# Macro tiles of 1024 x 2048 with 8 KB load rows in a quarter-turn kernel

## The chip, the cores and the metric

The kernel runs on one core of one Trainium2 chip (the other cores are not used by it). The metric is the device time of one execution in microseconds (us). Each kernel was run several times; medians are given with their range. All runs named here were in the fast state. The profile is one traced execution. Ratios are the mean time of one kernel's fast runs over that of the other's fast runs of the same rounds, so they are not quite the ratio of the medians that are quoted.

## The reference

```python
x = np.random.randn(8192, 8192).astype(np.float32);  k = 1
def reference(x, k):
    return np.rot90(x, k)          # out[i, j] = x[j, 8191 - i]
```

That is a transpose with the output rows in reverse order: 268 MB are read and 268 MB are written, and nothing is computed.

## The kernel before

It works in macro tiles, that is, blocks of the matrix that are loaded, transposed and stored together; here they have 1024 rows x 1024 columns. Each is loaded as two tiles of 2 MB, VectorE reverses the columns within each block of 128, TensorE transposes blocks of 128 x 128 into PSUM (the memory that TensorE writes to), ScalarE copies PSUM to an output tile, and ScalarE's queue stores 2 MB at a time. Both directions move rows of 1024 floats, that is, contiguous runs of 4 KB.

```python
QT = 4; PT = 4; S = 512; K = 2
a_pool, r_pool, o_pool: bufs=3 each, tiles of 2 MB;  psum_pool: bufs=2
for RB2 in range(n_rb2):
    for CB2 in range(n_cb2):
        ar_list = []
        for t in range(K):
            a_big = a_pool.tile([P, QT, K * S], dt, tag="a_big")
            src = x[r_base + t*S : r_base + (t+1)*S, c_base : c_base + K*S].rearrange("(q r) c -> r q c", q=QT)
            nc.sync.dma_start(out=a_big[:], in_=src)
            ar_big = r_pool.tile([P, QT, K * S], dt, tag="ar_big")
            nc.vector.tensor_copy(out=ar_big..., in_=a_big...[:, :, ::-1])      # cut
            ar_list.append(ar_big)
        for s in range(K):
            o_big = o_pool.tile([P, PT, K * S], dt, tag="o_big")
            for t in range(K):
                ... 16 transposes into psum_t ...                               # cut
                nc.scalar.copy(o_big[:, :, t*S : (t+1)*S], psum_t[:])
            nc.scalar.dma_start(out=dst, in_=o_big[:])
```

Of the kernel before, what the change touches and what calls it, by code (L numbers as in the profile page):

```python
# [1 line left out]

# [5 lines left out]

P = 128  # L10


@with_exitstack
def kernel(
    ctx: ExitStack,
    tc: tile.TileContext,
    x: bass.AP,
    k: bass.AP,
    out: bass.AP,
):  # L20
    nc = tc.nc
    assert k == 1, f"only k=1 supported, got {k}"

    N, M = x.shape
    dt = x.dtype

    QT = 4
    PT = 4
    S = 512
    K = 2  # L30

    n_rb2 = N // (K * S)
    n_cb2 = M // (K * S)

    consts = ctx.enter_context(tc.tile_pool(name="consts", bufs=1))
    ident = consts.tile([P, P], dt)
    make_identity(nc, ident)

    a_pool = ctx.enter_context(tc.tile_pool(name="a_pool", bufs=3))
    r_pool = ctx.enter_context(tc.tile_pool(name="r_pool", bufs=3))  # L40
    o_pool = ctx.enter_context(tc.tile_pool(name="o_pool", bufs=3))
    psum_pool = ctx.enter_context(tc.tile_pool(name="psum", bufs=2, space=bass.MemoryType.PSUM))

    for RB2 in range(n_rb2):
        for CB2 in range(n_cb2):
            c_base = CB2 * K * S
            r_base = RB2 * K * S

            ar_list = []
            for t in range(K):  # L50
                a_big = a_pool.tile([P, QT, K * S], dt, tag="a_big")
                src = x[
                    r_base + t * S : r_base + (t + 1) * S, c_base : c_base + K * S
                ].rearrange("(q r) c -> r q c", q=QT)
                nc.sync.dma_start(out=a_big[:], in_=src)  # L55

                ar_big = r_pool.tile([P, QT, K * S], dt, tag="ar_big")
                nblk = QT * K * S // P
                rev_src = a_big.rearrange("r q (b m) -> r (q b) m", m=P)[:, :, ::-1]
                nc.vector.tensor_copy(  # L60
                    out=ar_big.rearrange("r q (b m) -> r (q b) m", m=P),
                    in_=rev_src,
                )
                ar_list.append(ar_big)

            for s in range(K):
                cb = K * CB2 + s
                o_big = o_pool.tile([P, PT, K * S], dt, tag="o_big")
                for t in range(K):
                    psum_t = psum_pool.tile([P, PT, QT * P], mybir.dt.float32)  # L70
                    ar_big = ar_list[t]
                    for p in range(PT):
                        w = PT - 1 - p
                        col0 = s * S + p * P
                        for q in range(QT):
                            nc.tensor.transpose(  # L76
                                psum_t[:, w, q * P : (q + 1) * P],
                                ar_big[:, q, col0 : col0 + P],
                                ident,
                            )  # L80
                    nc.scalar.copy(o_big[:, :, t * S : (t + 1) * S], psum_t[:])  # L81

                top = N - S - cb * S
                dst = out[top : top + S, r_base : r_base + K * S].rearrange(
                    "(p m) f -> m p f", p=PT
                )
                nc.scalar.dma_start(out=dst, in_=o_big[:])


# [1 line left out]
_INS = ['x', 'k']  # L91
_OUTS = [((8192, 8192), 'float32')]
#: Inputs that are plain numbers.
_NUMBERS = {'k': 1}


# [26 lines left out]
```

## Time and profile before

| | before |
|---|---|
| time, median of 4 runs | 1285.98 us (1285.63 to 1286.27) |
| DMA rate in mid-kernel | 421 GB/s, engines full in every slice but the last |
| busy: TensorE, ScalarE, VectorE | 56%, 37%, 23% |
| load packets, store packets | 65,536 and 65,536 of 4 KB |

These are lines of the page of the kernel before. DMA is the busy share of the 16 DMA engines in 40 slices, in tenths; GB/s is what they moved; then come packets, queues (q1 is the load queue, q10 the store queue), the chain of waits by line, groups of instructions (busy us, mean ns; idle time before them and what ended it), and the DMA issues (number, size, median us from issue to landing).

```profile
DMA  9999999999999999999999999999999999999998
GB/s 382 422 421 421 421 421 422 421 421 421 421 421 421 421 421 421 421 422 421 420 421 421 421 421 421 421 421 421 422 420 420 421 421 422 421 421 421 421 421 361
DMA packets 135208, 537.48 MB, mean 418 GB/s; under 512 B 4096, under 2 KB 4096, under 8 KB 135168
...
q1 hardware_dynamic: 67584, 268.44, 50.9%
q10 hardware_dynamic: 67584, 268.44, 50.9%
...
DMA a_big<-in_x_dram 88%; DVE ar_big L60 8%; PE psum_t L76 2%; ACT o_big L81 1%; DVEq L60 0%; SPq L55 0%
...
L81 ACT COPY o_big<-psum_t 128x2048 f32<-128x2048 f32 x256 | 469.9, 1868 | 801.5 <-DMA out_dram<-o_big 771.6
L60 DVE COPY ar_big<-a_big 128x4096 f32<-128x4096 f32 x128 | 293.6, 2294 | 970.6 <-DMA a_big<-in_x_dram 816.4
...
a_big<-in_x_dram SPq DMA_DIRECT2D x128, 2048.0 KB, 27.4
out_dram<-o_big ACTq DMA_DIRECT2D x128, 2048.0 KB, 26.1
```

The reader should see that no slice of the DMA line is below 9 until the last, that the engines which compute wait for transfers for most of the time, and that both queues carry the same number of packets. The DMA engines bound the kernel.

The end of the kernel before, as stretches of 4 us (columns: busy us and number of instructions of PE, PEld, DVE, ACT and POOL, then granted TensorE clock, DMA share, GB/s):

```profile
1262.00:1266.00 4.00, 1.66 (x11) 1.69 (x12) 2.19 (x1) 1.87 (x1) 0.00 (x0) 0.88 1.02 421
1266.00:1270.00 4.00, 4.00 (x28) 4.00 (x27) 0.00 (x0) 2.13 (x2) 0.00 (x0) 0.69 0.72 297
1270.00:1274.00 4.00, 1.44 (x14) 1.21 (x12) 0.00 (x0) 3.37 (x2) 0.00 (x0) 1.00 1.00 407
```

There is a hole at 1266 to 1270 us: the last loads have landed, and the blocks that they brought are still being transposed (PE busy all 4.00 us), so there is too little to store.

### The profile page before, as it was taken

What the parts mean: (1) busy time and instruction counts of PE and PEld (TensorE: products, weight loads), DVE (VectorE), ACT (ScalarE), POOL (GpSimd) and SP (SyncE); (2) the same over time, 40 slices, a digit from 0 to 9 for tenths busy, and PEclk for the clock granted to TensorE, in tenths of its full rate; (3) what the DMA queues carried; (4) which work ended last, traced back from release to release, by engine and by line L of the source; (5) the groups of instructions that cost most, each with busy time, mean ns of one, the idle gap of its engine ahead of it and who ended that gap; (6) DMA issues with size and microseconds to landing.
All of it is one profiled execution on the core that took longest, in us unless ns stands there. A gap on an engine that the chain in (4) does not pass through costs nothing.

```text
span 1284.6 us, 9394 instructions
## 1 busy us (share of the span) xinstructions
PE 718.8 (56%) x4096; PEld 662.7 (52%) x4096; DVE 293.6 (23%) x128; ACT 471.1 (37%) x257; POOL 0.7 (0%) x6
## 2 busy tenths in 40 slices
PE   5465564556555565456554565555646556465553
PEld 5455464555544555456454464555645456455553
DVE  2222222222222222222222222222222222222221
ACT  3334433343333433343333433334333343334433
POOL 0000000000000000000000000000000000000000
PEclk9666766776767767776777767767677766776776
DMA  9999999999999999999999999999999999999998
GB/s 382 422 421 421 421 421 422 421 421 421 421 421 421 421 421 421 421 422 421 420 421 421 421 421 421 421 421 421 422 420 420 421 421 422 421 421 421 421 421 361
DMA packets 135208, 537.48 MB, mean 418 GB/s; under 512 B 4096, under 2 KB 4096, under 8 KB 135168
## 3 DMA queue, kind: packets, MB, share of 16 engines
q1 hardware_dynamic: 67584, 268.44, 50.9%
q10 hardware_dynamic: 67584, 268.44, 50.9%
q8 instruction: 32, 0.52, 0.1%
q14 instruction: 8, 0.07, 0.0%
HBM read 268.44 MB, written 268.44 MB: 418 GB/s over the span
## 4 chain that ended last, share of the span: by engine, by line
DMA 88%; DVE 8%; PE 2%; ACT 1%; issue 0%; DVEq 0%; SPq 0%
DMA a_big<-in_x_dram 88%; DVE ar_big L60 8%; PE psum_t L76 2%; ACT o_big L81 1%; DVEq L60 0%; SPq L55 0%
## 5 line engine op out<-in xcount | busy, mean ns | idle before, releaser
L76 PE MATMUL psum_t<-ident,ar_big 128*128 128x128 f32 x4096 | 718.8, 354 | 552.7 <-ACT o_big L81 354.4
L76 PEld LDWEIGHTS psum_t<-ident,ar_big 128*128 128x128 f32 x4096 | 662.7, 188 | 608.5 <-ACT o_big L81 389.5
L81 ACT COPY o_big<-psum_t 128x2048 f32<-128x2048 f32 x256 | 469.9, 1868 | 801.5 <-DMA out_dram<-o_big 771.6
L60 DVE COPY ar_big<-a_big 128x4096 f32<-128x4096 f32 x128 | 293.6, 2294 | 970.6 <-DMA a_big<-in_x_dram 816.4
L81 ACT ACT_TABLE_LOAD x1 | 1.3, 1283 | 0.7 <-PEq L104 0.7
masks.py:199 POOL TENSOR_SCALAR_AFFINE_SELECT ident<-ident 128x128 f32<-128x128 f32 x1 | 0.3, 292 | 0.1
masks.py:197 POOL MEMSET ident<- 128x128 f32 x1 | 0.2, 204 | 0.3 <-POOLq L104 0.3
L104 POOL MEMSET const-bfloat16-1.0<- 128x1 bf16 x1 | 0.1, 102 | 0.0
L104 POOL MEMSET const-uint8-127<- 128x1 uint8 x1 | 0.1, 102 | 0.0
L104 POOL MEMSET const-float32-0.0<- 128x1 f32 x1 | 0.1, 98 | 0.2 <-issue 0.2
L104 POOL MEMSET const-float32-1.0<- 128x1 f32 x1 | 0.1, 98 | 0.0
## 6 DMA issues: line engine op xcount, KB each, us to landing
a_big<-in_x_dram SPq DMA_DIRECT2D x128, 2048.0 KB, 27.4
out_dram<-o_big ACTq DMA_DIRECT2D x128, 2048.0 KB, 26.1
```

What stands on the lines that cost most here:

```text
L60: nc.vector.tensor_copy(out=ar_big.rearrange("r q (b m) -> r (q b) m", m=P), in_=rev_src,)
L76: nc.tensor.transpose(psum_t[:, w, q * P : (q + 1) * P], ar_big[:, q, col0 : col0 + P], ident,)
L81: nc.scalar.copy(o_big[:, :, t * S : (t + 1) * S], psum_t[:])
L104: nc = _bacc.Bacc("TRN2", target_bir_lowering=False, num_devices=1)
```

## The change

The intent: load rows of 8 KB (2048 floats) in place of 4 KB, in 1 MB transfers through a short staging ring of three tiles; keep 16 reversed row tiles (two macro tiles); store 2 MB as before, in rows of 4 KB. The diff, cut to its core:

```diff
+R = 1024
+C = 2048
+RT = R // P        # 8 row tiles of 1 MB
+G = 4096 // R
+PW = 2048 // R
-    r_pool = ctx.enter_context(tc.tile_pool(name="r_pool", bufs=3))
+    r_pool = ctx.enter_context(tc.tile_pool(name="r_pool", bufs=2 * RT))
...
-            for t in range(K):
-                a_big = a_pool.tile([P, QT, K * S], dt, tag="a_big")
-                src = x[...].rearrange("(q r) c -> r q c", q=QT)
-                nc.sync.dma_start(out=a_big[:], in_=src)
+            for t in range(RT):
+                a = a_pool.tile([P, C], dt, tag="a")               # bufs=3
+                nc.sync.dma_start(out=a[:], in_=x[r0 + t * P : r0 + (t + 1) * P, c0 : c0 + C])
+                ar = r_pool.tile([P, C], dt, tag="ar")
+                nc.vector.tensor_copy(out=ar..., in_=a...[:, :, ::-1])
+                rows.append(ar)
...
+            for g0 in range(0, CG, G):
+                o = o_pool.tile([P, G, R], dt, tag="o")            # bufs=3
+                for h in range(0, G, PW):
+                    ... 16 transposes into ps ...
+                    nc.scalar.copy(o[:, G - PW - h : G - h, :], ps[:])
+                nc.scalar.dma_start(out=dst, in_=o[:])
```

More of the change, by code (lines that the diff above doesn't have):

```diff
@@ L10 @@
 P = 128
+R = 1024
+C = 2048
+RT = R // P
+CG = C // P
+G = 4096 // R
+PW = 2048 // R
 @with_exitstack
@@ L25 @@
     dt = x.dtype
-    QT = 4
-    PT = 4
-    S = 512
-    K = 2
-    n_rb2 = N // (K * S)
-    n_cb2 = M // (K * S)
     consts = ctx.enter_context(tc.tile_pool(name="consts", bufs=1))
@@ L39 @@
     a_pool = ctx.enter_context(tc.tile_pool(name="a_pool", bufs=3))
-    r_pool = ctx.enter_context(tc.tile_pool(name="r_pool", bufs=3))
+    r_pool = ctx.enter_context(tc.tile_pool(name="r_pool", bufs=2 * RT))
     o_pool = ctx.enter_context(tc.tile_pool(name="o_pool", bufs=3))
-    psum_pool = ctx.enter_context(tc.tile_pool(name="psum", bufs=2, space=bass.MemoryType.PSUM))
-    for RB2 in range(n_rb2):
-        for CB2 in range(n_cb2):
-            c_base = CB2 * K * S
-            r_base = RB2 * K * S
-            ar_list = []
-            for t in range(K):
-                a_big = a_pool.tile([P, QT, K * S], dt, tag="a_big")
-                src = x[
-                    r_base + t * S : r_base + (t + 1) * S, c_base : c_base + K * S
-                ].rearrange("(q r) c -> r q c", q=QT)
-                nc.sync.dma_start(out=a_big[:], in_=src)
-                ar_big = r_pool.tile([P, QT, K * S], dt, tag="ar_big")
-                nblk = QT * K * S // P
-                rev_src = a_big.rearrange("r q (b m) -> r (q b) m", m=P)[:, :, ::-1]
+    psum_pool = ctx.enter_context(
+        tc.tile_pool(name="psum", bufs=2, space=bass.MemoryType.PSUM)
+    )
@@ L60 @@
+    for r0 in range(0, N, R):
+        for c0 in range(0, M, C):
+            rows = []
+            for t in range(RT):
+                a = a_pool.tile([P, C], dt, tag="a")
+                nc.sync.dma_start(
+                    out=a[:], in_=x[r0 + t * P : r0 + (t + 1) * P, c0 : c0 + C]
+                )
+                ar = r_pool.tile([P, C], dt, tag="ar")
                 nc.vector.tensor_copy(
-                    out=ar_big.rearrange("r q (b m) -> r (q b) m", m=P),
-                    in_=rev_src,
-                )
@@ L64 @@
-                ar_list.append(ar_big)
-            for s in range(K):
-                cb = K * CB2 + s
-                o_big = o_pool.tile([P, PT, K * S], dt, tag="o_big")
-                for t in range(K):
-                    psum_t = psum_pool.tile([P, PT, QT * P], mybir.dt.float32)
-                    ar_big = ar_list[t]
-                    for p in range(PT):
-                        w = PT - 1 - p
-                        col0 = s * S + p * P
-                        for q in range(QT):
+                    out=ar.rearrange("r (b m) -> r b m", m=P),
@@ L76 @@
+                    in_=a.rearrange("r (b m) -> r b m", m=P)[:, :, ::-1],
+                )
+                rows.append(ar)
+            for g0 in range(0, CG, G):
+                o = o_pool.tile([P, G, R], dt, tag="o")
+                for h in range(0, G, PW):
+                    ps = psum_pool.tile([P, PW, R], mybir.dt.float32)
+                    for w in range(PW):
+                        col = (g0 + h + w) * P
+                        for t in range(RT):
                             nc.tensor.transpose(
-                                psum_t[:, w, q * P : (q + 1) * P],
@@ L78 @@
-                                ar_big[:, q, col0 : col0 + P],
+                                ps[:, PW - 1 - w, t * P : (t + 1) * P],
+                                rows[t][:, col : col + P],
                                 ident,
                             )
-                    nc.scalar.copy(o_big[:, :, t * S : (t + 1) * S], psum_t[:])
-                top = N - S - cb * S
-                dst = out[top : top + S, r_base : r_base + K * S].rearrange(
-                    "(p m) f -> m p f", p=PT
+                    nc.scalar.copy(o[:, G - PW - h : G - h, :], ps[:])
@@ L86 @@
+                top = M - c0 - (g0 + G) * P
+                dst = out[top : top + G * P, r0 : r0 + R].rearrange(
+                    "(g m) f -> m g f", g=G
                 )
-                nc.scalar.dma_start(out=dst, in_=o_big[:])
+                nc.scalar.dma_start(out=dst, in_=o[:])
 _INS = ['x', 'k']
```

## The prediction

> **What bounds it now.** The DMA engines. The page's slices show them at 9 in every slice, 421 GB/s nearly throughout; TensorE is busy 56%, ScalarE 37%, VectorE 23%. The chain of waits is 88% loads, and the longest waits of the compute engines name transfers (VectorE 816 us for loads, ScalarE 772 us for stores). So 536.9 MB / 421 GB/s = 1275 us, plus some 9 us of start and end. Compute changes are free while neither queue runs dry.
>
> **What the change does to DMA.** Bytes stay. Stores keep their form: 128 of 2 MB in 4 KB rows. Loads go from 128 of 2 MB in 4 KB rows to 256 of 1 MB in 8 KB rows. In the trace's packet records a 4 KB packet takes 159 ns, and steady flow passes one per about 155 ns and engine (421 GB/s / 16), so neighbours overlap by some 4 ns. The few 8 KB packets there are (instruction fetches) take 309 ns undisturbed, not 318. So a packet costs about 9 ns plus 27.3 GB/s, of which about 5 ns are exposed; one 8 KB packet for two of 4 KB saves about 5 ns, an estimate. The Trainium skill ("DMA: Bandwidth & Descriptors", Why small descriptors are slow) states a fixed overhead of about 3 cycles per packet; the trace agrees in size.
>
> - Removed: 32,768 load packets, 2,048 per engine x 5 ns = **-10.2 us**.
> - Added: 128 load completions, a 4-byte packet of 9 ns per engine each: **+0.6 to 1.2 us**.
> - Moved: in the last 20 us the rate falls to 297 GB/s for 4 us while the last transposes catch up. The new buffers (16 reversed row tiles, 3 in staging: 19 MB) let loads run ahead, so the end should be stores back to back: **-1 us**.
> - Packets alternate between queues. If loads get 8 KB for each 4 KB of stores, loads run ahead, then block on reversed tiles while stores flow alone. Loads alone looked slower (packets near 164 ns in the 16 us before the first stores), stores alone did not (159 ns): **+0 to 5 us**, estimated.
>
> **Compute.** Transposes stay 4096, evictions 256 of 128x2048 (1.87 us). VectorE goes from 128 copies of 2.29 us to 256 of half the size, about 1.17 us: +6 us in total, hidden. The staging ring is short, but a refill needs the 1.2 us copy, a wait and 2 us of latency, while two more loads of 2.5 us (full rate) or 5 us (shared) are queued. Transposes of a macro tile wait for 8 loads, but a second macro tile is buffered. Three output tiles hold 15 us of stores at full rate, as before.
>
> All packet savings lie on the critical path, since the engines never rest.
>
> **Prediction: 1277 us, 1269 to 1287 in 8 of 10.** Faster by over 2%: 0.03; within 2%: 0.91; slower by over 2%: 0.06.
>
> **What would show it.** Right: 32,768 load packets of 8 KB at about 309 ns, about 104,500 packets in all, DMA 9 in all slices, 424 to 425 GB/s in the middle, first store near 28 us without a dip, no hole before the last stores, copies of 1.17 us. Wrong: still 65,536 load packets (rows split at 4 KB): then about 1285 us. Load packets well over 320 ns, or dips of the DMA slices every 40 us: slower.
>
> **What would make it wrong.** Stores starved by larger load packets so that single-queue stretches run below 421 GB/s; 8 KB packets held up in HBM or SBUF; a refill of the short ring slower than assumed, leaving the load queue empty when stores are blocked too.

## The result, and the profile after

The changed kernel took 1281.35 us (median of 4 runs, 1279.48 to 1283.95) against 1285.98 us beside it: ratio 0.9965, 95% interval 0.995 to 0.998. It is 4.6 us faster, within the predicted range and within 2%, but half of the 9 us that was expected. Its runs scatter over 4.5 us; those of the kernel before over 0.6 us.

Lines of the page of the changed kernel that answer to those above:

```profile
DMA  9999999999999999999999999999999999999998
GB/s 387 419 423 425 423 424 423 423 425 424 423 424 423 425 423 423 421 423 418 425 423 422 423 424 423 418 424 423 424 414 424 423 422 416 424 423 421 419 407 359
DMA packets 104492, 537.52 MB, mean 420 GB/s; under 512 B 6144, under 2 KB 6144, under 8 KB 71680
...
q10 hardware_dynamic: 67584, 268.44, 51.2%
q1 hardware_dynamic: 36864, 268.45, 49.9%
...
DMA out_dram<-o 86%; ACT o L76 10%; DMA a<-in_x_dram 2%; PE ps L71 1%; DVE ar L58 0%; ACTq L82 0%; ACTq L76 0%; SPq L52 0%
...
L58 DVE COPY ar<-a 128x2048 f32<-128x2048 f32 x256 | 308.8, 1226 | 932.4 <-DMA a<-in_x_dram 526.1
...
a<-in_x_dram SPq DMA_DIRECT2D x256, 1024.0 KB, 10.4
out_dram<-o ACTq DMA_DIRECT2D x128, 2048.0 KB, 24.7
```

Load packets fell to 32,768 (36,864 less 4,096 completion packets, the small packets that report a transfer as done) and the rate of most slices rose to 423 to 425 GB/s, but some sag to 418, 416, 414 and 407, which none before did. The chain now follows the stores: loads run ahead, and stores are what ends last.

### Where the time went: a budget from the packet records

Every DMA packet's start and duration are in the trace. The commonest duration is 84 ns for 2 KB, 159 ns for 4 KB and 309 ns for 8 KB. From these records the span is split into four parts: *start and end* (before the first and after the last data packet); *idle* (fewer than 16 packets in flight, the missing ones added up and divided by 16); *stretch* (what packets took beyond the commonest duration of their size, divided by 16); and the rest, the *nominal flow*, which is the time of the bytes and of the fixed cost of the packets. Each profile is one run, so that a part can differ by some us between two profiles of the same kernel. The records do not name the engine, so an engine without work can count as stretch rather than idle time, if another has two packets open at once: the two parts are not cleanly separable.

| run | median us | span of the profiled run | nominal flow | stretch | idle | start and end |
|---|---|---|---|---|---|---|
| before | 1285.98 | 1284.6 | 1275.3 | 2.6 | 3.7 | 3.0 |
| changed | 1281.35 | 1281.3 | 1266.2 | 7.7 | 4.4 | 2.9 |
| changed, again (e0_after) | 1279.97 | 1278.2 | 1266.2 | 4.9 | 4.3 | 2.9 |
| e1_load4k | 1294.40 | 1293.2 | 1275.8 | 4.3 | 10.1 | 3.0 |
| e2_ring2 | 1285.43 | 1283.3 | 1266.1 | 8.1 | 6.2 | 2.9 |
| e3_out4 | 1282.78 | 1282.4 | 1266.1 | 8.4 | 5.0 | 2.9 |
| e4_both8k | 1316.50 | 1311.4 | 1257.5 | 45.5 | 5.5 | 2.9 |
| e5_ring32 | 1280.93 | 1279.1 | 1266.1 | 5.2 | 5.0 | 2.9 |
| e6_rev10 | 1288.17 | 1288.9 | 1266.2 | 10.1 | 9.8 | 2.9 |
| e7_load2k | 1348.09 | 1343.9 | 1297.0 | 27.3 | 16.6 | 3.0 |
| e8_ring5 | 1280.80 | 1280.1 | 1266.1 | 5.6 | 5.4 | 2.9 |
| e9_both8k_ring5 | 1294.35 | 1292.1 | 1257.1 | 27.0 | 5.0 | 3.0 |
| e10_shared | 1421.05 | 1418.8 | 1257.5 | 31.8 | 126.6 | 2.9 |
| e11_quarters | 1280.84 | 1277.6 | 1256.8 | 7.4 | 10.4 | 3.0 |

The change took 9.1 us off the nominal flow, and gave back 2.3 to 5.1 us in stretch and under 1 us in idle time.

### Where packets stretch in the changed kernel

Loads get two thirds of the bytes while both queues are full: between 1223 and 1235 us, about 33 load packets of 8 KB and 37 store packets of 4 KB start in each us. So loads run ahead until the 16 reversed tiles are full, and at each macro-tile boundary the load queue is empty for 3 to 10 us (30 such pauses in this profile, mean 7.9 us); the kernel before has none over 3 us. Two restarts of the loads, as stretches of 4 us (columns as above), the first clean and the second not:

```profile
1010.00:1014.00 4.00, 2.47 (x20) 2.23 (x18) 2.25 (x2) 1.42 (x1) 0.00 (x0) 0.93 1.03 423
1014.00:1018.00 4.00, 3.50 (x32) 3.46 (x32) 1.25 (x2) 2.21 (x2) 0.00 (x0) 1.00 1.04 430
1018.00:1022.00 4.00, 1.47 (x9) 1.24 (x7) 0.95 (x1) 3.16 (x2) 0.00 (x0) 0.85 1.01 424
```

```profile
1210.00:1214.00 4.00, 3.97 (x27) 3.73 (x26) 0.75 (x1) 2.09 (x2) 0.00 (x0) 0.75 1.02 415
1214.00:1218.00 4.00, 3.74 (x32) 3.46 (x32) 2.75 (x3) 2.45 (x3) 0.00 (x0) 1.00 1.01 353
1218.00:1222.00 4.00, 2.61 (x24) 2.57 (x25) 0.00 (x0) 3.11 (x2) 0.00 (x0) 1.00 1.02 350
1222.00:1226.00 4.00, 1.13 (x11) 0.89 (x9) 1.23 (x1) 0.00 (x0) 0.00 (x0) 0.95 1.02 424
```

In the second, the DMA share stays over 1.00 while the rate falls to 353 and 350 GB/s: the engines have packets, but the packets take longer. In the us from 1217 the median store packet took 319 ns in place of 159, and in the next us the longest load packet took 1160 ns in place of 309. Of the 4.5 us of stretch within -3 to +6 us of the 30 restarts, 4.1 us fall to the 14 pauses longer than 8.5 us. But the first stretched store of this restart starts at 1216.6 us, when the loads had been issued (from 1214.5 us) and none of their packets had started (the first does at 1218.1 us). In the five restarts with more than 0.4 us of stretch, 1.7 of 3.7 us lie before the first load packet, so that competing load data cannot be the whole cause.

### The end

The last stretches of the changed kernel:

```profile
1268.00:1272.00 4.00, 0.00 (x0) 0.00 (x0) 0.00 (x0) 1.34 (x1) 0.00 (x0) 0.75 1.02 412
1272.00:1276.00 4.00, 0.00 (x0) 0.00 (x0) 0.00 (x0) 0.00 (x0) 0.00 (x0) 0.50 1.03 414
1276.00:1280.00 4.00, 0.00 (x0) 0.00 (x0) 0.00 (x0) 0.00 (x0) 0.00 (x0) 0.50 0.20 82
```

The hole before the last stores is gone, as predicted. But the engines do not end together. Data packets in flight, from the packet records, every half us:

```
changed: 1276.0:17 1276.5:5 1277.0:3 1277.5:3 1278.0:2 1278.5:1 1279.0:1 1279.5:1 1280.0:1 1280.5:0
before:  1280.5:16 1281.0:9 1281.5:9 1282.0:5 1282.5:1 1283.0:1 1283.5:0
```

Idle time from 1230 us on is 3.1 us before and 3.2 us after. The 16 completion packets of one 2 MB store come further apart as a run goes on: from first to last, 1.6 us in the first eighth of the stores and 5.8 us in the last eighth, in the kernel before. What sets the engines apart was not looked for.

### The profile page after: what moved, and what is told of

Its sections match the earlier page's. It is cut to its first block, busy times and chain, and to the rows that moved or that the text cites. A ratio compares the mean times of both kernels' runs of the same rounds, so it can differ in the third digit from the quotient of the medians.

```text
span 1281.3 us, 9827 instructions
## 1 busy us (share of the span) xinstructions
PE 626.6 (49%) x4096; PEld 591.1 (46%) x4096; DVE 308.8 (24%) x256; ACT 466.9 (36%) x257; POOL 0.7 (0%) x6
## 2 busy tenths in 40 slices
DMA packets 104492, 537.52 MB, mean 420 GB/s; under 512 B 6144, under 2 KB 6144, under 8 KB 71680
## 3 DMA queue, kind: packets, MB, share of 16 engines
q1 hardware_dynamic: 36864, 268.45, 49.9%
## 4 chain that ended last, share of the span: by engine, by line
DMA 88%; ACT 10%; PE 1%; issue 1%; DVE 0%; ACTq 0%; SPq 0%
DMA out_dram<-o 86%; ACT o L76 10%; DMA a<-in_x_dram 2%; PE ps L71 1%; DVE ar L58 0%; ACTq L82 0%; ACTq L76 0%; SPq L52 0%
## 5 line engine op out<-in xcount | busy, mean ns | idle before, releaser
L71 PE MATMUL ps<-ident,ar 128*128 128x128 f32 x4096 | 626.6, 326 | 639.6 <-ACT o L76 619.9
L71 PEld LDWEIGHTS ps<-ident,ar 128*128 128x128 f32 x4096 | 591.1, 172 | 674.9 <-ACT o L76 650.2
L76 ACT COPY o<-ps 128x2048 f32<-128x2048 f32 x256 | 465.6, 1870 | 801.8 <-DMA out_dram<-o 755.9
L58 DVE COPY ar<-a 128x2048 f32<-128x2048 f32 x256 | 308.8, 1226 | 932.4 <-DMA a<-in_x_dram 526.1
## 6 DMA issues: line engine op xcount, KB each, us to landing
a<-in_x_dram SPq DMA_DIRECT2D x256, 1024.0 KB, 10.4
```

Of the source, the lines that this page charges most:

```text
L58: nc.vector.tensor_copy(out=ar.rearrange("r (b m) -> r b m", m=P), in_=a.rearrange("r (b m) -> r b m", m=P)[:, :, ::-1],)
L71: nc.tensor.transpose(ps[:, PW - 1 - w, t * P : (t + 1) * P], rows[t][:, col : col + P], ident,)
L76: nc.scalar.copy(o[:, G - PW - h : G - h, :], ps[:])
```

## The experiments

The first theory: the packet saving is real and of the predicted size; about half is given back where the load queue restarts after a pause. Rivals: the gain comes from the deeper buffers and not from the packets (R2); stretch is noise of the chip (R1); the short staging ring starves the engines (T2, formed after the 2048 x 2048 run).

Some expectations below need a correction. When those of e4_both8k, e10_shared and e11_quarters were written, the budget counted the idle time ahead of the first data packet twice, which made every nominal flow 12 to 13 us too small. The differences between runs were not touched, but "about 1245 us" should read 1257 us, and the times expected there were some 12 us too low. Stretch and idle are unaffected apart from that. Even so corrected, the faster of the two times expected was missed in all three.

**e0_after: the changed kernel again.** No edit.

> The changed kernel again, beside the others on one chip. Theory (T): the packet saving of about 10 us is there, and about half of it is given back where the load queue is dry for 5 to 10 us at each macro-tile boundary and packets stretch when it restarts, plus a few engines that end 3 us after the rest. T expects 1279 to 1284 us, and stretched packets again only at restarts, 3 to 8 us per engine in total. Rival R1 (stretching is noise of the chip, not tied to restarts): stretched packets spread over the whole span, in the kernel before as much as here. Rival R2 (the gain came from deeper buffers, not from packet size) says nothing of this run.

1279.97 us (5 runs, 1278.82 to 1282.81), ratio 0.9954 (0.9942 to 0.9967). Nominal flow is again 1266.2 us; stretch was 4.9 us, of which 1.7 us near restarts, and only one pause was longer than 8.5 us. So the restarts are not the whole of the stretch, but they go with the profile that had more of it. R1 is not refuted by this: most of the stretch here lies away from restarts, though the kernel before has 2.6 us in all.

**e1_load4k: only the packet size undone.**

```diff
-  a = a_pool.tile([P, C], dt, tag="a")
+  a = a_pool.tile([P, 2, C // 2 + 16], dt, tag="a")     # a 64-byte hole after each 4 KB
-  nc.sync.dma_start(out=a[:], in_=x[...])
+  nc.sync.dma_start(out=a[:, :, : C // 2], in_=x[...].rearrange("r (h c) -> r h c", h=2))
```

> Only the packet size of the loads is undone: the staging tile has a 64-byte hole after each 4 KB, so a row arrives as two packets of 4 KB; everything else is the changed kernel. T: 65,536 load packets, shares of loads and stores equal while both run, no long load-queue pauses in mid-kernel, stretched packets under 3 us per engine; 1285 to 1288 us. R2: the time stays near 1281. R1: stretched packets as many as in the changed kernel, and 1289 to 1293 us.

1294.40 us (1293.88 to 1294.97), ratio 1.0064: slower than the kernel before, and beyond what any theory had put down. Loads went back to 4 KB packets:

```profile
DMA packets 137260, 537.52 MB, mean 416 GB/s; under 512 B 6144, under 2 KB 6144, under 8 KB 137216
```

Nominal flow rose by 9.6 us against the changed kernel, which for 2,048 packets more per engine is 4.7 ns a packet, so the packet term of the prediction holds. The hole itself did no harm that shows: load packets took 159.4 ns in the mean, as in the kernel before, and VectorE's copies 1.23 us, as in the changed kernel. Stretch fell slightly. What nobody had counted is the end:

```profile
1256.00:1260.00 4.00, 0.47 (x1) 0.18 (x1) 0.67 (x1) 0.00 (x0) 0.00 (x0) 0.50 1.03 422
1260.00:1264.00 4.00, 2.14 (x10) 2.14 (x11) 1.23 (x1) 0.00 (x0) 0.00 (x0) 0.50 0.69 285
1264.00:1268.00 4.00, 4.00 (x25) 4.00 (x24) 0.00 (x0) 2.51 (x2) 0.00 (x0) 0.62 0.03 14
1268.00:1272.00 4.00, 3.38 (x29) 2.91 (x28) 0.00 (x0) 3.49 (x3) 0.00 (x0) 1.00 0.47 194
1272.00:1276.00 4.00, 3.59 (x33) 3.32 (x32) 0.00 (x0) 3.49 (x3) 0.00 (x0) 1.00 1.03 420
```

With equal packets loads no longer run ahead (last load 1259.9 us, against 1239.3 us with 8 KB), so when the last row lands no stores are queued, and the engines rest until the last macro tile is transposed: 9.1 us of idle time at the end against 3.2 us. R2 is refuted: the new macro tiles and buffers without the large packets make the kernel slower than the one before, by 0.64%. The large load packets pay twice, once in fixed cost and once by giving loads the lead.

**e2_ring2: a shorter staging ring.**

```diff
-  tc.tile_pool(name="a_pool", bufs=3)
+  tc.tile_pool(name="a_pool", bufs=2)
```

> Staging ring of two tiles in place of three: a load is issued only when the load before it is the only one in flight, which should hold loads back from taking two thirds of the engines. T: load-queue pauses at the boundaries shorter than 4 us, stretched packets below 4 us per engine, 1274 to 1279 us. Against T (short refills leave engines idle, or restarts of any kind stretch packets): 1283 us or more, with more stretched packets than before.

1285.43 us (1284.09 to 1287.13), ratio 0.9996. There were only 10 pauses over 3 us, of 4.3 us in the mean, with 0.3 us of stretch near them, as the theory said. But the time did not fall, for the first 40 us, when loads run alone, suffered. The same stretch in four runs, in the order e2_ring2, changed kernel, e5_ring32, e8_ring5:

```profile
0.00:40.00 40.00, 17.38 (x104) 13.51 (x105) 14.40 (x12) 11.43 (x7) 0.70 (x6) 1.00 0.91 337
```

```profile
0.00:40.00 40.00, 19.26 (x126) 15.65 (x127) 15.96 (x13) 12.20 (x7) 0.70 (x6) 1.00 0.96 389
```

```profile
0.00:40.00 40.00, 19.45 (x123) 15.69 (x124) 15.96 (x13) 12.30 (x7) 0.70 (x6) 1.00 0.94 376
```

```profile
0.00:40.00 40.00, 19.83 (x126) 15.97 (x127) 15.95 (x13) 12.30 (x7) 0.70 (x6) 1.00 0.97 397
```

The last figure is the rate: 337 GB/s with a ring of two, 389 with three, 376 where the third tile serves the first two macro tiles only, and 397 with five.

**e3_out4: a fourth output tile.**

```diff
-  tc.tile_pool(name="r_pool", bufs=2 * RT)
+  tc.tile_pool(name="r_pool", bufs=2 * RT - 2)       # for room
-  tc.tile_pool(name="o_pool", bufs=3)
+  tc.tile_pool(name="o_pool", bufs=4)
```

> Four output tiles in place of three and 14 reversed row tiles in place of 16. If packets stretch because the store queue is nearly dry when the loads restart, a fourth 2 MB store in the queue takes that away: stretched packets below 4 us per engine and 1275 to 1279 us. If the restart of the loads alone does it: stretched packets as in the changed kernel, 1279 to 1284 us.

1282.78 us (1280.31 to 1284.18), ratio 0.9973. There were 30 pauses as before, and 5.5 us of stretch near restarts, 5.3 us of it after the 13 pauses over 8.5 us. A fourth store in the queue does not help, so this speaks against a store queue near its end as the cause, though two reversed tiles had to go for it.

**e4_both8k: 8 KB rows both ways.**

```diff
-R = 1024
+R = 2048
-  tc.tile_pool(name="r_pool", bufs=2 * RT)
+  tc.tile_pool(name="r_pool", bufs=RT + 2)
-  tc.tile_pool(name="o_pool", bufs=3)
+  tc.tile_pool(name="o_pool", bufs=4)
+  macros = [...]                  # cut; so are the loops, which now run over this list
+  r0, _, c0 = macros.pop()        # the last macro tile in two halves of 1024 rows
+  macros += [(r0, R // 2, c0), (r0 + R // 2, R // 2, c0)]
-  o = o_pool.tile([P, G, R], dt, tag="o")
+  o = o_pool.tile([P, 2048], dt, tag="o")        # 1 MB
```

> Macro tiles of 2048 x 2048, so that stores go in 8 KB rows as well (the last macro tile in two halves of 1024 rows); three staging tiles, 18 reversed row tiles, four 1 MB output tiles. If a packet costs about 5 ns of exposed time whichever queue it is on, the nominal flow falls by another 9 to 10 us against the changed kernel: 1264 to 1272 us with some more idle and stretch, since only two reversed tiles are spare and loads and stores take turns. If stores gain nothing from larger packets, or the turns leave the engines idle: 1280 us or more.

1316.50 us (1313.21 to 1328.08), ratio 1.0255: 2.5% slower. The nominal flow did fall, by another 8.7 us to 1257.5 us, so packets cost the same on the store queue. But the reversed tiles hold one macro tile only, loads and stores take turns, and 39 us of stretch came up in load packets.

**e5_ring32: a ring of two, with a third tile for the start.**

```diff
+  f_pool = ctx.enter_context(tc.tile_pool(name="f_pool", bufs=1))
-  a = a_pool.tile([P, C], dt, tag="a")
+  early = r0 == 0 and c0 < 2 * C and t % 3 == 2
+  a = (f_pool if early else a_pool).tile([P, C], dt, tag="a")        # a_pool: bufs=2
```

> The ring of two tiles, but with a third staging tile while the first two macro tiles load, where the ring of two lost some 6 us (337 GB/s, load packets stretched). If that loss was the whole reason why the ring of two did not gain: 1277 to 1281 us, rate of the first 40 us as in the changed kernel. If short pauses of the loads cut the stretching (theory T): stretched packets of the middle below 3 us. If not: 3 us or more, and no faster than the changed kernel.

1280.93 us (1280.71 to 1281.92), ratio 0.9962. The loss at the start was what had held the ring of two back. Pauses are fewer (14 over 3 us, mean 3.8 us), stretch near restarts is 0.03 us and that of the middle (40 to 1230 us) 2.9 us, just under the 3 us that had been put down; the runs scatter over 1.2 us in place of 4. But the median is no lower than that of the changed kernel (1279.97 and 1281.35 us in its two series). Away from restarts, the stretch of the middle was 2.8 us, against 1.4 and 0.6 us in the two profiles of the changed kernel: what went at the restarts came back in part elsewhere. So the smaller scatter goes with the missing long pauses, which five runs do not prove, and taking these away is worth no time that these runs can show.

**e6_rev10: fewer reversed tiles.**

```diff
-  tc.tile_pool(name="r_pool", bufs=2 * RT)
+  tc.tile_pool(name="r_pool", bufs=RT + 2)
```

> Ten reversed row tiles in place of 16, so the load queue is dry for longer at each of the macro-tile boundaries. If stretching comes with restarts after long pauses (T): more stretched packets, 8 us or more in the middle, or idle engines, 1284 us or more. If stretching is independent of pauses: 2 to 6 us as before, and the time within 2 us of the changed kernel.

1288.17 us (1282.58 to 1290.72), ratio 1.0002. The pauses grew to 9.2 us in the mean, stretch of the middle to 7.6 us (just under the 8 expected). But only 3.5 us of it lie near restarts, less than the 4.5 us of the changed kernel, although 16 of the 31 pauses are longer than 8.5 us, and some last 13 to 16 us: the length of a pause alone does not set the stretch, against the first theory. Idle time at the end grew to 8.1 us, since loads cannot run as far ahead (last load at 1256.8 us). The larger part of the loss is the end, not the restarts.

**e7_load2k: the dose.**

```diff
-  a = a_pool.tile([P, C], dt, tag="a")
+  a = a_pool.tile([P, 4, C // 4 + 16], dt, tag="a")     # otherwise as e1_load4k, with h=4
```

> Dose of the packet cost: the staging tile has a hole after each 2 KB, so a row arrives as four packets of 2 KB (131,072 load packets). At 5 ns per packet the nominal flow of the engines rises by 20 us against the run with 4 KB load packets, and stores, with twice the bytes per turn, run dry, so idle time at the end grows: 1312 to 1330 us. If the packet has no fixed cost and only the order of turns matters: 1295 to 1302 us.

1348.09 us (1345.65 to 1349.18), ratio 1.048, slower than expected.

```profile
DMA packets 202796, 537.52 MB, mean 400 GB/s; under 512 B 6144, under 2 KB 6144, under 8 KB 202752
```

The nominal flow rose by 21.2 us against e1_load4k: 4,096 more packets per engine at 5.2 ns each, where 20 us was expected. The miss is in stretch (27.3 us) and idle (16.6 us): stores now move more bytes than loads while both queues are full (67 packets of 4 KB a us to 68 of 2 KB) and run dry, so loads ran alone (over 90% of the bytes, in steps of half a us) for 331 us of the span, against 35 us in the changed kernel.

**e8_ring5: the changed kernel with five staging tiles.**

```diff
-  tc.tile_pool(name="a_pool", bufs=3)
+  tc.tile_pool(name="a_pool", bufs=5)
-  tc.tile_pool(name="r_pool", bufs=2 * RT)
+  tc.tile_pool(name="r_pool", bufs=2 * RT - 2)
```

> The changed kernel with five staging tiles and 14 reversed ones (look-ahead of 19 tiles as before). New theory (T2), formed on the 2048 x 2048 run: load packets stretch where loads run alone and only three 1 MB loads can be in flight, since a refill waits for the slowest engine, the copy and the issue; stretch is starved engines, not a cost of restarts. T2 expects the stretch of the first 40 us to fall from 1.5 to 1.9 us to under 1 us, that of the middle to under 2 us, and 1274 to 1279 us. If the restart itself stretches packets: no less stretch in the middle, 1279 to 1284 us.

1280.80 us (1278.85 to 1283.77), ratio 0.996. The stretch of the first 40 us fell to under 1 us as T2 said, but that of the middle was 3.5 us, and the time stayed. For this change the short ring costs about 1 us, at the start; T2 does not explain the rest.

**e9_both8k_ring5: 2048 x 2048 with five staging tiles.** Against e4_both8k:

```diff
-  tc.tile_pool(name="a_pool", bufs=3)
+  tc.tile_pool(name="a_pool", bufs=5)
-  tc.tile_pool(name="r_pool", bufs=RT + 2)
+  tc.tile_pool(name="r_pool", bufs=RT)
```

> 2048 x 2048 macro tiles with five staging tiles and 16 reversed ones, in place of three and 18. T2: the load stretch of 39 us in the middle falls under 12 us, and the time to 1266 to 1284 us. If loads alone are slow in themselves (memory read without writes beside it), stretch stays over 25 us and the time over 1300 us.

1294.35 us (1292.82 to 1295.19), ratio 1.0065: 22 us faster than e4_both8k by the change of the ring alone (its two tiles more came from the reversed ones), though not as fast as T2 had it. The same 24 us, with loads alone on the engines, in e4_both8k and in e9_both8k_ring5:

```profile
104.00:128.00 24.00, 6.20 (x18) 2.61 (x18) 11.16 (x10) 1.15 (x1) 0.00 (x0) 0.50 1.00 388
```

```profile
104.00:128.00 24.00, 6.75 (x21) 3.15 (x22) 11.04 (x9) 2.47 (x2) 0.00 (x0) 0.50 1.01 424
```

388 GB/s with three transfers of 1 MB to be in flight, 424 with five. So in these runs loads alone are not slow in themselves; three are too few where no stores fill the gaps. Stretch in load packets of the middle fell from 39.0 to 16.4 us, not to under 12; in stores it rose from 4.5 to 9.7 us. Of these 26 us, 18.8 us lie near the 15 restarts, each after some 28 us without loads (6.0 us in e4_both8k, whose pauses are as long). So T2 fits the loads alone, and not what happens when both queues fill again.

**e10_shared: one pool of nine tiles for loads and stores.** Against e4_both8k:

```diff
-  a_pool (bufs=3), o_pool (bufs=4), r_pool (bufs=RT + 2)
+  s_pool (bufs=9), r_pool (bufs=RT)
-  a = a_pool.tile([P, C], dt, tag="a")
+  a = s_pool.tile([P, C], dt, tag="s")
-  o = o_pool.tile([P, 2048], dt, tag="o")
+  o = s_pool.tile([P, 2048], dt, tag="s")
```

> 2048 x 2048 macro tiles with one pool of nine 8 KB tiles that loads and output tiles take in turn, and 16 reversed tiles, so that up to nine loads or stores are in flight. T2: load stretch under 10 us, nominal flow about 1245 us, 1255 to 1272 us, faster than both kernels. If loads alone are slow in themselves: over 1290 us.

1421.05 us (1419.63 to 1422.26), ratio 1.1051. The time failed altogether, although load stretch (5.6 us) did fall under 10 us and nominal flow was as expected. Tiles of one pool come free in program order, so a load had to wait for a store of the macro tile before: the load queue waited 1190 us in all for stores to land, and the engines were idle for 127 us. This run tests its own pool order and says nothing of the question.

**e11_quarters: 2048 x 2048 without turns.** The reversed rows lie in 64 tiles of [128, 512]; those of a quarter of the columns come free once it is transposed, and the next macro tile's rows take them in that order. Five staging tiles, four output tiles.

```diff
+  free = [r_pool.tile([P, QC], dt, name=f"q{i}", tag=f"q{i}") for i in range(RT * NQ)]
...
+  quarters = [free.pop(0) for _ in range(NQ)]           # for each row tile: four reversing copies
...
+  free += [rows[t][q] for t in range(RT)]               # after quarter q is transposed
```

> 2048 x 2048 macro tiles with five staging tiles, but the reversed rows lie in 64 quarter tiles of 2 KB per partition that come free a quarter of the columns at a time, so the next macro tile can load while this one is stored. The packet cost gives a nominal flow of about 1245 us as in the other 2048 x 2048 runs. If what those lost (stretch of 26 to 45 us) came from loads and stores taking turns, each alone on the engines with few transfers in flight, stretch falls under 10 us and the time to 1254 to 1266 us, over 1.5% faster than the kernel before and faster than the changed one. If large packets both ways stretch by themselves: stretch over 20 us, 1275 us or more.

1280.84 us (1279.37 to 1281.25), ratio 0.996. Stretch fell to 7.4 us from 45.5 and 27.0 us, under the 10 expected: so what the 2048 x 2048 runs had lost went with the turns of loads and stores. The time expected, 1254 to 1266 us (1266 to 1278 us with the correction), was missed. Nominal flow is 1256.8 us, 9.4 us under that of the changed kernel. The time is not lower, for the idle time more than doubled, to 10.4 us. Its end, in stretches of 4 us:

```profile
1212.00:1216.00 4.00, 0.00 (x0) 0.00 (x0) 0.00 (x0) 1.83 (x2) 0.00 (x0) 0.68 0.93 389
...
1220.00:1224.00 4.00, 3.47 (x29) 3.11 (x27) 2.99 (x9) 1.67 (x1) 0.00 (x0) 0.96 0.57 240
1224.00:1228.00 4.00, 0.33 (x1) 0.14 (x1) 1.22 (x4) 1.86 (x1) 0.00 (x0) 0.89 0.74 305
1228.00:1232.00 4.00, 2.79 (x13) 2.79 (x14) 1.43 (x4) 1.87 (x1) 0.00 (x0) 0.50 0.58 242
1232.00:1236.00 4.00, 4.00 (x30) 4.00 (x29) 0.00 (x0) 2.40 (x2) 0.00 (x0) 0.76 0.55 225
```

From 1217 to 1228 us only one or two load packets start in each us, as one engine would do that shares its turns with stores: it seems that one engine ended its loads some 12 us after the rest, and the last macro tile could not be transposed before. The trace does not name engines, so this is a reading, not shown.

Two more versions did not build: reversing the row order on the store's side of the transfer, and reading the transposed operand back to front, either of which was to make VectorE's copy needless.

No version tried was clear of the changed kernel: e5_ring32, e8_ring5 and e11_quarters all have a ratio of 0.996 to the kernel before, as it has itself. What the runs show is where the missing half went, mostly into stretched packets; what stretches them they do not show. The restarts of the loads, the first theory, are a part of it at most.

## Why the prediction was right or wrong, point by point

- **What bounds the kernel: right.** The DMA engines are at 9 in all slices but the last, before and after.
- **Packet cost, -10.2 us and +0.6 to 1.2 us: right.** Nominal flow fell by 9.1 us, where the two terms give 9.0 to 9.6. Packets were 32,768 of 8 KB at 309 ns (mean 310.9), 104,492 in all. Undoing only this (e1_load4k) and doubling it (e7_load2k) gave 4.7 and 5.2 ns a packet. The Trainium skill ("DMA: Bandwidth & Descriptors", Why small descriptors are slow) states about 3 cycles per packet; at the 850 MHz of the same page (Where 436 GB/s comes from) that is 3.5 ns, an estimate, which takes that clock to be the one that the cycles are counted in; the page does not say so. The runs show about 5 ns exposed, and the measurement decides.
- **Shares of the queues: right.** "If loads get 8 KB for each 4 KB of stores, loads run ahead, then block on reversed tiles while stores flow alone." They did, with 30 pauses. The same page (Queues, rings and completion order) says that an engine takes turns between queues packet by packet; 33 load packets to 37 store packets a us agree. With load packets of 4 KB (e1_load4k) it is 51 to 52 and with 2 KB (e7_load2k) 68 to 67, medians over the us in which both queues start packets.
- **"+0 to 5 us" for the load-heavy time: the term that was mis-sized.** The forecast of 1277 us left 1 to 2 us of it. Stretch grew by 5.1 us in one profile and 2.3 us in another. The reason given, that loads alone are slower, is at most a small part: in the changed kernel they are alone for about 35 us only, and the first 40 us have 1.6 us of stretch, against 1.1 us before. The stretch lies in part near restarts of the loads (4.5 of 7.7 us in one profile, 1.7 of 4.9 us in the other); its cause stays open.
- **"-1 us" at the end: the hole went, the gain did not come.** Idle time from 1230 us on is 3.2 us after 3.1 before, for the engines end up to 4 us apart. The prediction did not see that this term was not small but hung on the packet size: without the lead that large packets give to loads, the new macro tiles cost 9 us of idle time at the end.
- **Short ring: right that it holds in mid-kernel.** A longer ring gained 0.6 us of stretch at the start and no time; a ring of two cost 4 to 5.5 us.
- **Copies of 1.17 us: near (1.23). First store near 28 us: issued at 30.25 us.** "424 to 425 GB/s in the middle" is near: the slices without restarts that stretch show 421 to 425, most of them 423 or 424.

What stays open: why packets stretch at some restarts and not at others with pauses as long (in the changed kernel the slow ones all come after about 490 us, in e9_both8k_ring5 from the first on), and why they stretch before the first load packet and away from restarts; and what sets the 16 engines apart.

## What to carry to other kernels

Where the DMA engines never rest, count packets: doubling the contiguous run from 4 to 8 KB was worth about 5 ns for each packet saved, 0.7% of this kernel for one direction, and an estimate from the commonest packet durations of the trace was good to about 1 us. The two queues started nearly equal numbers of packets, so the larger packet also decided which queue ran ahead; check that it is the one whose lead you need at the end. Half of the saving in the steady flow did not arrive, so sum up stretched packets and idle engines as well as bytes.

## What the Trainium skill lacked or had wrong

- "Perfetto Trace Analysis" (DMA Optimizations) says that batching small transfers into larger ones, its example being 2 KB into 4 KB or 8 KB, can improve throughput dramatically; it gives no amounts. Here, with two full queues, 1 MB transfers and only the contiguous runs of the loads changed, 2 KB, 4 KB and 8 KB gave 1348.09, 1294.40 and 1281.35 us: 4.0% from the first step and 1.0% from the second.
- "DMA: Bandwidth & Descriptors" (Why small descriptors are slow) gives about 3 cycles per packet, without the clock (3.5 ns by the estimate above); durations of 84, 159 and 309 ns for 2, 4 and 8 KB show 9 ns, of which 4.7 to 5.2 ns are exposed when packets follow on one another.
- The same page says that queues take turns by packet, not what follows: with 8 KB against 4 KB packets one queue got about 1.8 times the other's bytes, which filled the buffers, made 30 pauses of 3 to 10 us, and decided 6 us of idle time at the end.
- No page read says how many transfers must be in flight when one direction runs alone: with 1 MB loads through a staging copy of 1.23 us, three gave 388 GB/s and five 424 over the same 24 us.
- No page read gives how far apart the 16 engines end, or how that grows in a long kernel: the completions of one 2 MB store spread from 1.6 us (first eighth of the run) to 5.8 us (last eighth) in the kernel before.
